# Two model blocks in fp32r on one core: the splits of the weights get the priority of instructions 400 places earlier

## Chip, cores and metric

The kernel runs on one core of one Trainium2 chip, in one launch. The metric is the device time of one execution in microseconds (us), lower is better. It is stated as the median over several runs.

## The reference

The program computes four layers of depth over 256 tokens of width 1024, in fp32. The first block has a state-space layer (SSD), a differential attention layer and a convolutional feed-forward network behind each of them; the second block has four gated feed-forward networks, a memory attention with a gated convolution in the first of its layers, and a forgetting attention with memory attention in the second. Cut to its skeleton:

```python
def first_block(x, ...):
    for i in range(2):
        h = rmsnorm(x, norm_mix_g[i])
        x = x + (ssd_mixer(h, ...) if i == 0 else diff_attention(h, ...))
        x = x + conv_ffn(rmsnorm(x, norm_ffn_g[i]), ...)      # D_FF = 2816
    return x

def second_block(x, mem, ...):
    mem_n = rmsnorm_2(mem, mem_norm)
    for l in range(2):
        # l == 1: keys, values and forget gates of x are made first
        x = x + 0.5 * swiglu(rmsnorm_2(x, ffn_norm[l, 0]), ...)  # D_FF_2 = 2816
        proj = rmsnorm_2(x, mix_norm[l]) @ w
        x = x + concatenate([token_mixer(proj), memory_attention(proj, mem_n)]) @ w_out
        x = x + 0.5 * swiglu(rmsnorm_2(x, ffn_norm[l, 1]), ...)
    return rmsnorm_2(x, final_norm)
```

Nearly all of the work is activations (256 x 1024) times weights. All weights together are about 309 MB in fp32, each used once.

## The kernel before

Activations lie transposed in SBUF, features on the partitions and the 256 tokens along a row. Every weight matmul is done in three: `mm3` (L252) multiplies the high half of the weights with the high half of the activations, the high half with the low half, and the low half with the high half, and adds all three up in one PSUM bank. For that each raw weight tile has to be split. `load` and `load_tiles` (L228, L233) issue one DMA from SP into a raw buffer `wr` (three of them, 2048 columns each). `split` (L240) then makes two tiles from 1024 columns of it or fewer: `wh`, a copy rounded to fp32r by ScalarE (ACT), and `wl`, the difference of raw and `wh`, by VectorE (DVE) or, in the state-space layer, every fourth time by GpSimd (POOL). `wh` and `wl` have five buffers each. A raw buffer is free again when all its low halves are made; a `wh` or `wl` buffer when the last matmul that reads it is through.

Three loops use this. `lin_T` (L290) takes two tiles of 128 output features at a time, 8 matmul triples each, into one of three PSUM buffers `psA`, and has it evacuated (for the state-space layer: DVE multiplies by the row norm, L394, ACT and DVE run a convolution of four taps, L886 and L889). `lin_N` (L315) makes outputs with tokens on the partitions. `lin_out` (L338) is the way back to 1024 features; it adds onto `X` (L366) and feeds the next norm.

The state-space layer has, per group of eight heads, a chain beside these loops: transposes on PE (L768), a copy `xn` (ACT, L770), decay factors `E` (PE L785, DVE L792, ACT L797, POOL L798), small matmuls (L815), the sum `y` (DVE L834), and then a gate with its own norm (POOL L842, ACT L843, POOL L384, DVE L850), transposes (L858) and the split of the result `yy` (L865, L866), which `lin_out` reads. The attention layer has rope chains (L993 to L1009) and heads (L1021 on).

These chains are generators. A running count `net.now` of estimated PE time says where in the source order each of their pieces is issued (`spawn`, `adv`, `resume`). That order gives each instruction a place number, its priority. A planner then goes through the program in a model of the machine and gives each engine, whenever it comes free there, the instruction with the lowest number among those that can run: inputs made, and a buffer free for the output. What comes out is one fixed list per engine, which the chip works through in order. So the number is a preference among what can run at the moment, not a place in the list.

Of the kernel before, what the change touches and what calls it, by code (L numbers as in the profile page):

```python
# [10 lines left out]
F32 = mybir.dt.float32  # L11
# [3 lines left out]
AF = mybir.ActivationFunctionType  # L15
ALU = mybir.AluOpType
# [84 lines left out]
class Net:  # L101
# [138 lines left out]
    def split(self, raw, c0, n):  # L240
        nc = self.nc
        hi = self.t(self.wh, [128, 1024], F32R, "wh")
        lo = self.t(self.wh, [128, 1024], F32R, "wl")
        nc.scalar.activation(out=hi[:, :n], in_=raw[:, c0:c0 + n], func=AF.Copy)  # L244
        self.cnt += 1
        pool = self.share and self.cnt % self.share == 0 and (self.norm is None or self.norm.done)
        eng = nc.gpsimd if pool else nc.vector
        eng.tensor_tensor(out=lo[:, :n], in0=raw[:, c0:c0 + n],  # L248
                          in1=hi[:, :n].bitcast(F32), op=ALU.subtract)
        return hi, lo  # L250

    def mm3(self, ps, wh, wl, xh, xl, first, last):  # L252
# [118 lines left out]
    def make_norm(self, gname, split=True, sq="act", pool=None, base=64):  # L371
        return Norm(self, gname, split, sq, self.xp if pool is None else pool, base)
# [30 lines left out]
class Norm:  # L403
    def __init__(self, net, gname, split, sq, pool, base):
        self.n, self.g, self.split = net, gname, split
        self.done = False
        self.sq = sq
        self.keep = None
        self.wait = 4.5
        self.acc = net.t(net.s2, [128, S], F32, "nacc")  # L410
        if split:
            self.xh, self.xl = Moving(net, pool, KD, "xx", base, (0,)).parts()
# [102 lines left out]
def next_norm(net, gname, split=True, pool=None, base=64):  # L515
    box = {}

    def after(m):
        if m == 0:
            box["n"] = net.make_norm(gname, split=split, pool=pool, base=base)  # L520
        box["n"].step(m)
    return box, after
# [1025 lines left out]
```

## Time and profile before

| | |
|---|---|
| median of 3 runs | 1797.99 us (1792.98 to 1803.73) |
| profiled execution, its own time | 1808.89 us |
| its span, first to last instruction | 1807.2 us |
| PE, DVE, ACT, POOL busy | 98%, 68%, 56%, 27% |
| mean granted TensorE clock | 0.994 |

Times in the rows are microseconds from the start of the span. PE is TensorE's matmuls, PEld its weight loads. Matmuls are pipelined and their ends are modelled, so that a busy PE can still run below its best rate; the number of matmuls in a stretch says more. A square bracket at the end of a row gives how long the engine was idle just before the instruction, and what ended that.

### The profile page before, as it was taken

The page shows a single profiled execution, that of the slowest core. Times are in us where ns is not written, and L with a number is a line of the kernel's source. Part 1 is how long each engine was busy: PE and PEld are TensorE (multiplying, and loading weights), DVE is VectorE, ACT ScalarE, POOL GpSimd, SP SyncE. Part 2 cuts the span into 40 slices and gives each one's busy share as a digit, 9 for nine tenths or more (in the row PEclk, how much of TensorE's full clock was granted, in tenths as well). Part 3 has the DMA queues.
Part 4 walks back from the last instruction along what each step waited for, and adds up shares of the span by engine and source line. Part 5 has one row for each costly group of instructions (what it writes and reads, how often), then busy time and mean ns, then how long its engine had stood idle before and what let it go on. Part 6 is the DMA issues. An engine that isn't in the chain of part 4 may idle for free.

```text
span 1807.2 us, 34773 instructions
## 1 busy us (share of the span) xinstructions
PE 1774.4 (98%) x14067; PEld 1708.8 (95%) x14067; DVE 1235.2 (68%) x1863; ACT 1015.7 (56%) x1661; POOL 490.9 (27%) x453
## 2 busy tenths in 40 slices
PE   8999999999999999999999999999999999999997
PEld 7887999998789999999999999999999998999997
DVE  6998789867777997655567775556655567575553
ACT  7667576646666665554455454455544455564443
POOL 3555234402111442043201223310043210023321
PEclk9999999999999999999999999999999999999999
DMA  6332655465226555655464475556555454265553
GB/s 233 118 139 81 212 178 186 158 195 206 94 100 228 187 180 162 208 199 187 152 221 143 140 233 187 180 163 199 195 199 186 157 206 164 82 222 187 180 162 103
DMA packets 76497, 312.12 MB, mean 173 GB/s; under 512 B 6192, under 2 KB 6320, under 8 KB 72624
## 3 DMA queue, kind: packets, MB, share of 16 engines
q1 hardware_dynamic: 76304, 309.89, 50.4%
q8 instruction: 111, 1.82, 0.4%
q14 instruction: 50, 0.41, 0.1%
q0 software_dynamic: 32, 0.00, 0.0%
HBM read 308.82 MB, written 1.05 MB: 171 GB/s over the span
## 4 chain that ended last, share of the span: by engine, by line
PE 86%; DVE 6%; POOL 2%; ACT 1%; issue 1%; DMA 1%; DVEq 0%; ACTq 0%; POOLq 0%
PE psA L254 26%; PE psA L256 25%; PE psA L255 25%; PE psA L329 2%; PE psA L327 2%; PE psA L328 2%; DVE wl L248 2%; DVE cvy L889 2%; POOL rs L384 1%; PE psM L1033 1%; ACT wh L244 0%; DVE E L792 0%; PE psM L1147 0%; PE psY L1178 0%; DMA wr<-memT 0%
## 5 line engine op out<-in xcount | busy, mean ns | idle before, releaser
L248 DVE TENSOR_TENSOR wl<-wr,wh 128x1024 fp32r<-128x1024 f32 (+3 forms) x651 | 719.7, 1108 | 389.9 <-ACT wh L244 387.2
L244 ACT ACTIVATE wh<-wr 128x1024 fp32r<-128x1024 f32 (+3 forms) x660 | 628.1, 955 | 491.4 <-PE psA L255 313.3
L256 PE MATMUL psA<-xx,wl 128*128 128x256 f32 x2752 | 775.6, 282 | 5.9 <-DVE wl L248 5.9
L254 PE MATMUL psA<-xx,wh 128*128 128x256 f32 x2752 | 779.7, 283 | 0.2 <-DVE pad L394 0.2
L255 PE MATMUL psA<-xx,wh 128*128 128x256 f32 x2752 | 773.6, 281 | 0.1
L256 PEld LDWEIGHTS psA<-xx,wl 128*128 128x128 f32 x2752 | 526.4, 191 | 7.4 <-DVE wl L248 6.9
L254 PEld LDWEIGHTS psA<-xx,wh 128*128 128x128 f32 x2752 | 518.8, 189 | 1.8 <-issue 0.5
L255 PEld LDWEIGHTS psA<-xx,wh 128*128 128x128 f32 x2752 | 518.5, 188 | 1.1 <-issue 0.5
L256 PE MATMUL psA<-gg,wl 128*128 128x256 f32 x1056 | 296.9, 281 | 0.0
L254 PE MATMUL psA<-gg,wh 128*128 128x256 f32 x1056 | 296.6, 281 | 0.0
L255 PE MATMUL psA<-gg,wh 128*128 128x256 f32 x1056 | 296.4, 281 | 0.0
L544 POOL TENSOR_TENSOR p<-s,t 128x256 f32<-128x256 f32 x132 | 184.0, 1394 | 367.8 <-ACT s L572 367.8
L256 PEld LDWEIGHTS psA<-gg,wl 128*128 128x128 f32 x1056 | 202.1, 191 | 0.0
L254 PEld LDWEIGHTS psA<-gg,wh 128*128 128x128 f32 x1056 | 198.2, 188 | 0.0
L255 PEld LDWEIGHTS psA<-gg,wh 128*128 128x128 f32 x1056 | 198.2, 188 | 0.0
L431 POOL TENSOR_TENSOR nacc<-nacc,sq 128x256 f32<-128x256 f32 x72 | 63.3, 879 | 487.2 <-ACT sq L376 486.4
L547 POOL TENSOR_TENSOR gg<-p,gg 128x256 fp32r<-128x256 f32 x132 | 109.5, 830 | 125.5 <-ACT gg L546 125.5
L546 ACT ACTIVATE gg<-p 128x256 fp32r<-128x256 f32 x132 | 54.2, 412 | 127.0 <-POOL p L544 126.9
L254 PE MATMUL psA<-yy,wh 128*128 128x256 f32 x384 | 107.8, 282 | 0.1
L255 PE MATMUL psA<-yy,wh 128*128 128x256 f32 x384 | 106.9, 279 | 0.3 <-DVE yy L1223 0.3
L256 PE MATMUL psA<-yy,wl 128*128 128x256 f32 x384 | 106.6, 278 | 0.0
L394 DVE TENSOR_TENSOR t<-psA,R 128x512 f32<-128x512 f32 (+1 forms) x104 | 69.4, 670 | 36.9 <-PE psA L256 35.5
(291 smaller groups left out, 1921.8 us busy)
## 6 DMA issues: line engine op xcount, KB each, us to landing
wr<-up SPq DMA_DIRECT2D x132, 1024.0 KB, 4.8
wr<-dn SPq DMA_DIRECT2D x96, 704.0 KB, 4.0
wr<-w_a SPq DMA_DIRECT2D x14, 1024.0 KB, 4.8
wr<-w_ssd SPq DMA_DIRECT2D x12, 1024.0 KB, 5.1
wr<-w_ain SPq DMA_DIRECT2D x12, 1024.0 KB, 4.8
wr<-w_ssdo SPq DMA_DIRECT2D x16, 512.0 KB, 4.4
wr<-w_z SPq DMA_DIRECT2D x7, 1024.0 KB, 4.7
wr<-w_ao SPq DMA_DIRECT2D x16, 384.0 KB, 3.2
```

The lines of the kernel that those rows point to most:

```text
L244: nc.scalar.activation(out=hi[:, :n], in_=raw[:, c0:c0 + n], func=AF.Copy)
L248: eng.tensor_tensor(out=lo[:, :n], in0=raw[:, c0:c0 + n], in1=hi[:, :n].bitcast(F32), op=ALU.subtract)
L254: mm(ps, lhsT=wh, rhs=xh, start=first, stop=False)
L255: mm(ps, lhsT=wh, rhs=xl, start=False, stop=False)
L256: mm(ps, lhsT=wl, rhs=xh, start=False, stop=last)
L327: mm(ps[b], lhsT=xh[:, k, xs], rhs=hi[:, c], start=k == 0, stop=False)
L328: mm(ps[b], lhsT=xl[:, k, xs], rhs=hi[:, c], start=False, stop=False)
L394: self.nc.vector.tensor_tensor(out=o, in0=p, in1=self.bc(R, n), op=ALU.mult)
L431: eng.tensor_tensor(out=self.acc, in0=self.acc, in1=sq, op=ALU.add)
L544: nc.gpsimd.tensor_tensor(out=p, in0=s, in1=t[:, 1], op=ALU.mult)
L546: nc.scalar.activation(out=gh[:, j], in_=p, func=AF.Copy)
L547: nc.gpsimd.tensor_tensor(out=gl[:, j], in0=p, in1=gh[:, j].bitcast(F32), op=ALU.subtract)
```

## The change

The two instructions of a split are issued inside a block that lowers the running place number by 400 and sets it back afterwards. All else keeps its number. The line that makes `wh` moves below the two lines that choose the engine for `wl`; those lines issue nothing.

```diff
         hi = self.t(self.wh, [128, 1024], F32R, "wh")
         lo = self.t(self.wh, [128, 1024], F32R, "wl")
-        nc.scalar.activation(out=hi[:, :n], in_=raw[:, c0:c0 + n], func=AF.Copy)
         self.cnt += 1
         pool = self.share and self.cnt % self.share == 0 and (self.norm is None or self.norm.done)
         eng = nc.gpsimd if pool else nc.vector
-        eng.tensor_tensor(out=lo[:, :n], in0=raw[:, c0:c0 + n],
-                          in1=hi[:, :n].bitcast(F32), op=ALU.subtract)
+
+        with self.tc.high_priority(400):
+            nc.scalar.activation(out=hi[:, :n], in_=raw[:, c0:c0 + n], func=AF.Copy)
+            eng.tensor_tensor(out=lo[:, :n], in0=raw[:, c0:c0 + n],
+                              in1=hi[:, :n].bitcast(F32), op=ALU.subtract)
         return hi, lo
```

## Rows read from the trace of the kernel before

**Rows 1.** Page, part 1: busy us (share of the span) and instructions of each engine.

```profile
PE 1774.4 (98%) x14067; PEld 1708.8 (95%) x14067; DVE 1235.2 (68%) x1863; ACT 1015.7 (56%) x1661; POOL 490.9 (27%) x453
```

**Rows 2.** Stretches: length, busy us (count) of PE, PEld, DVE, ACT, POOL; PEclk, DMA.

```profile
28.00:170.00 142.00, 129.00 (x874) 115.47 (x874) 132.67 (x229) 100.34 (x151) 71.80 (x44) 0.96 0.33 116
...
400.00:575.00 175.00, 170.09 (x1040) 142.65 (x1039) 126.16 (x303) 110.27 (x244) 33.33 (x34) 0.99 0.43 152
575.00:950.00 375.00, 375.00 (x3187) 375.00 (x3187) 259.55 (x332) 209.90 (x324) 110.16 (x105) 1.00 0.55 188
```

**Rows 3.** Waits of PE: who waited for what: us in total, times, longest us.

```profile
PE psA L256 <- DVE wl L248: 5.9, 4, 2.4
PE psM L785 <- ACT xn L770: 4.4, 1, 4.4
PE psM L1013 <- DVE qt L1009: 3.7, 3, 2.2
...
PE psA L329 <- DVE wl L248: 1.6, 2, 1.3
```

**Rows 4.** Chain of waits from 28 to 191 us, shares by line.

```profile
by line: DVE cvy L889 16.7%; DVE wl L248 10.5%; issue 7.0%; PE psA L254 5.7%; PE psA L256 5.6%; PE psA L255 5.4%; DVE E L792 4.6%; POOL E L798 3.7%; POOL y L842 3.4%; POOL rs L384 2.9%; DVE pad L394 2.6%; PE psY L815 2.6%; PE psM L785 2.4%;
```

**Rows 5.** Timeline of ACT and DVE, 34 to 76 us: start, us, instruction, count.

```profile
34.67 3.89 ACT L244 ACTIVATE wh<-wr 128x1024 fp32r<-128x1024 f32 x4
...
43.45 1.22 DVE L248 TENSOR_TENSOR wl<-wr,wh 128x1024 fp32r<-128x1024 f32 x1
...
64.76 2.25 DVE L248 TENSOR_TENSOR wl<-wr,wh 128x1024 fp32r<-128x1024 f32 x1
66.94 5.59 DVE L889 SCALAR_TENSOR_TENSOR cvy<-pad,cv,cvy 128x256 f32<-128x256 f32 x6
72.46 2.35 DVE L248 TENSOR_TENSOR wl<-wr,wh 128x1024 fp32r<-128x1024 f32 x2
```

**Rows 6.** Waits over the whole span: ACT before a split.

```profile
ACT wh L244 <- PE psA L255: 313.3, 303, 4.1
```

**Rows 7.** Timeline of PE: instructions before which PE stood idle.

```profile
44.73 0.55 PE L256 MATMUL psA<-xx,wl 128*128 128x256 f32 x1 [2.36 <-DVE wl L248]
...
73.72 0.39 PE L256 MATMUL psA<-xx,wl 128*128 128x256 f32 x1 [1.67 <-DVE wl L248]
...
129.66 0.50 PE L785 MATMUL psM<-cc,sel 64*128 64x256 f32 x2 [4.43 <-ACT xn L770]
...
190.70 1.29 PE L858 MATMUL psM<-ident,y 128*128 128x128 f32 x8 [0.68 <-DVE y L850]
```

**Rows 8.** Stretches at a granted clock (PEclk) of 0.50.

```profile
44.79:48.21 3.42, 3.42 (x16) 3.42 (x17) 3.41 (x4) 2.60 (x5) 2.02 (x1) 0.50 0.24 43
130.13:136.95 6.82, 6.82 (x27) 5.92 (x27) 6.13 (x17) 2.66 (x4) 3.64 (x3) 0.50 0.31 131
```

**Rows 9.** Timeline of DVE: its idle time in the state-space layer.

```profile
94.58 2.31 DVE L775 TENSOR_TENSOR xdt<-xn,NT 128x512 f32<-128x512 f32 x2 [2.22 <-ACT xn L770]
...
137.85 0.87 DVE L792 TENSOR_SCALAR E<-psM,NT 128x128 f32<-128x128 f32 x3 [1.59 <-PE psM L785]
140.92 5.41 DVE L889 SCALAR_TENSOR_TENSOR cvy<-pad,cv,cvy 128x256 f32<-128x256 f32 x6 [2.21 <-ACT cvy L886]
```

**Rows 10.** Timeline of DVE, 164 to 185 us: the last group's chain.

```profile
164.63 4.21 DVE L792 TENSOR_SCALAR E<-psM,NT 128x128 f32<-128x128 f32 x16
...
175.82 0.88 DVE L850 TENSOR_SCALAR y<-y,rs 128x512 f32<-128x512 f32 x2 [4.43 <-POOL rs L384]
...
182.70 1.31 DVE L248 TENSOR_TENSOR wl<-wr,wh 128x1024 fp32r<-128x1024 f32 x1 [0.42 <-ACT wh L244]
183.93 1.27 DVE L834 TENSOR_TENSOR y<-psY,xn 128x512 f32<-128x512 f32 x2
```

**Rows 11.** Timeline of POOL: its products for E.

```profile
62.02 6.12 POOL L798 TENSOR_TENSOR E<-E,cbm 128x512 f32<-128x512 f32 x4
...
169.09 6.03 POOL L798 TENSOR_TENSOR E<-E,cbm 128x512 f32<-128x512 f32 x4
```

## Prediction

> **What bounds the kernel now.** I read the page's busy shares first. PE is busy for 1774.4 us, 98% of the span, and DVE for 1235.2 [rows 1]. The profiled execution took 1808.89 us, its span of 1807.2 and 1.7 us around it; that is 10.9 us above the median of the three timed runs, 1797.99. I work out differences in the profiled execution and take them off the median.
>
> Second, the stretches [rows 2]. From 575 to 950 us (two feed-forward blocks and more) PE has work all the time: 375.00 of 375 us, 3187 matmuls, one every 117.7 ns. There a split that comes earlier can give nothing. What PE lacks lies in a few places: 13.0 of the 142 us from 28 to 170 (the state-space layer), 4.9 of the 175 us of the attention layer. In the first of these DVE is busy for 132.67 of 142 us, its idle time 9.3 us.
>
> Third, who PE waited for [rows 3]. Only two rows name the low half of a split (wl, line 248): 5.9 us in four waits and 1.6 us in two, 7.5 us together. The largest single wait, 4.4 us, is for the copy xn of line 770; 3.7 us are for the rope chain of the attention layer (line 1009).
>
> Fourth, the chain of waits from 28 to 191 us [rows 4]. The three PE lines of the weight matmuls hold 16.7% of it together; DVE alone holds 16.7% with the convolution (L889), 10.5% with wl and 4.6% with E. So in this layer the end is set by DVE's total work more than by any one wait of PE.
>
> Fifth, how late the splits are there [rows 5]. ACT makes four high halves back to back from 34.67 to 38.56 us. Every fourth low half goes to POOL, so the second of these four, done at 36.6, is for DVE at the latest; DVE takes its next low half at 43.45, 6.8 us later, and PE stands until 44.73 for it [rows 7]. From 66.94 to 72.46 DVE runs six convolution instructions and only then the low halves that PE stands for at 73.72. DVE takes older work first, and the low halves stand behind it. In the saturated blocks it is the other way round: ACT itself stands idle before the split, 313.3 us in 303 waits, until PE frees a buffer [rows 6]. There the split is already the first thing to run when it can.
>
> **The change part by part.** No instruction is added or removed; every high half on ACT and every low half on DVE or POOL gets a number 400 lower. A tile of 1024 columns makes some 27 instructions (24 matmuls, two halves, a load), so 400 places are about 15 tiles, while the wh and wl pools hold 5. The number therefore means "first whenever it can run", and the pools are the limit. SP's loads keep their numbers; a raw buffer is freed earlier by as much as its low half comes earlier.
>
> *Saturated blocks.* The split is already first [rows 6] and PE has no gap [rows 2]: 0. An eviction may stand behind one split of 1.22 us, while the three psA buffers cover more than one tile pair (48 matmuls of 117.7 ns, 5.6 us). If that cover were gone it would cost 1.2 us a pair; I take 0.
>
> *State-space layer, what goes.* [...] The wait of 4.43 us at 129.66 and the half clock of 6.82 us behind it (3.4 us) have another cause, the order on ACT; they go only if that order happens to change [rows 7, 8].
>
> *What is late next.* PE gains nothing at the end of the layer by this alone. At 190.70 it has already run out of other work and waits 0.68 us for the last head group's gated output, y of line 850 [rows 7]. What PE wins before that point it gives back there, unless the DVE chain that makes y comes earlier too. So the layer must be priced on DVE. Three terms:
> - DVE's own idle time where PE or ACT was late: 2.22, 1.59 and 2.21 us [rows 9], 6.0 together. The first comes after PE's waits for wl up to then (the one at 73.72 among them), the others after its stand at 129.66 [rows 7]. With PE earlier they can shrink to 0: -6.0. Lower end 0, since the second and third come from the ACT order.
> - More splits ahead of the last group's E. If PE is 7.5 us further on, it has freed 7.5/2.8 = 2.7 tiles more (24 matmuls of 117.7 ns are 2.8 us), so three more low halves of 1.22 us run before the 16 instructions of E at 164.63 [rows 5, 10]: +3.7. Ends 0 and five buffers, 6.1.
> - The end of the chain. DVE stands 4.43 us before line 850 for POOL's reciprocal root, until 175.82; later y of line 834 starts only when a low half of 1.31 us that began at 182.70 is through [rows 10]. Splits that ran in that hole would not stand in front later: -1.3. Ends 0 and -1.3.
>
> Sum for this layer: -6.0 + 3.7 - 1.3 = -3.6 us.
>
> *Attention layer.* PE's waits are for the rope chain, not for splits [rows 3]. Two low halves put ahead of that chain would cost 2 x 1.22 = 2.4 us; PE coming later or earlier may save half of a half-clock stretch like the first, 1.7. I take 0, nearest to the row that shows no wait for wl there. *Start.* The first split waits for its load in any case; a later one (3.89/4 = 0.97 us on ACT [rows 5]) could get in front of the scaled input: 0 to +1.0, taken as 0, since the next raw tiles arrive behind the input.
>
> [...] A low half that began at 64.76 took 2.25 us against 1.22 for the one at 43.45, while POOL ran its E products from 62.02 to 68.14 [rows 5, 11]. [...]
>
> All in all: 1808.9 - 3.6 = 1805.3 as profiled, and 1798.0 - 3.6 = 1794 us as timed. The likeliest case's own range takes the ends: -6.0 - 1.3 - 1.7 = -9.0 (1789) and 3.7 + 2.4 + 1.0 = +7.1 (1805).
>
> **The rivals.**
> One, nothing moves: the planner's order already has each split in front where it matters. For it: the 303 waits of ACT for a buffer [rows 6]. Against: the low half that lay ready for 6.8 us [rows 5]. Time 1798.
>
> Two, faster: PE's gains are kept. The wl waits go (7.5), the first half clock goes (1.7), and the ACT order behind the stand at 129.66 changes as well (4.4 + 3.4): 17.0 us, 1781. For it: each of these is PE standing with work loaded. Against: DVE is 93% busy in that layer and PE has no slack at 190.70.
>
> Three, slower: the last head group's chain is pushed back. With splits first, all five buffers are filled before E at 164.63, 5 x 1.22 = 6.1 us, and POOL's four E products of 6.03 us at 169.09 [rows 11] and the gate follow that much later, with PE out of work. The same in the attention layer, where two low halves stand ahead of each of two rope chains, 4 x 1.22 = 4.9. Together +11.0: 1809. It decides from the point where the added splits exceed the 6.0 us of DVE idle time that can be regained, that is at five of them. For it: PE's waits at 190.70 and for line 1009 show chains without slack. Against: splits are limited by the buffers that PE frees, and the hole of 4.43 us can take three of them.
>
> [...]
>
> **How the numbers follow.** Forecast 0.42, rival one 0.10, two 0.23, three 0.21, four 0.04. A measurement of this kernel can tell about 0.5% from no change, 9.0 us: 1789.0 to 1807.0. Below it lie rival two and 0.03 of the forecast, 0.26. Inside lie rival one and 0.38 of the forecast, 0.48. Above lie three, four and 0.01 of the forecast, 0.26. The range of 8 in 10 reaches past rivals two and three, 1778 to 1813: the lower end is 1781 with 3 us of the waits for line 1009 gone too, the upper end falls just short of rival four.
>
> **What would show it.** Right: PE's waits for wl fall from 7.5 us to under 2; low halves start within some 1.5 us of their high halves from 28 to 170 us; DVE idles under 5 us there; PE's wait for line 850 at the layer's end grows from 0.68 us to several; the stretches from 575 us on keep PE at full. Wrong: the layer's end, the last transposes of line 858, moves by over 9 us either way, or PE gets gaps in a feed-forward block because an eviction stands behind a split.

## The result and the profile after

The change makes the kernel slower. After it takes 1815.07 us (median of 16 runs, 1801.76 to 1831.17), before 1792.45 us on the same chip (16 runs, 1781.66 to 1803.86): a ratio of 1.0122, 95% interval 1.0099 to 1.0146, or 18 to 26 us. (The ratio leaves out the run of 1831.17 us, which lies over 1.5% above the fastest of its kernel.) I had forecast 1794 us and a range up to 1813. The profiled execution of after happens to be the fastest of its 16 (1801.76 us, span 1800.0), that of before (1808.89 us) is slower than any of its 16. The two spans say nothing about the difference; it has to be read stage by stage.

Lines of the changed kernel stand mostly two further down than before: `wh` is L249, `wl` L250, the matmuls of `mm3` L256 to L258. Part 1 of its page:

```profile
PE 1752.1 (97%) x14067; PEld 1681.3 (93%) x14067; DVE 1232.5 (68%) x1863; ACT 1016.0 (56%) x1661; POOL 486.5 (27%) x453
```

The three stretches of [rows 2] in the trace of after, same columns:

```profile
28.00:170.00 142.00, 127.14 (x852) 114.71 (x850) 119.62 (x209) 90.81 (x137) 62.83 (x39) 0.94 0.33 117
400.00:575.00 175.00, 165.46 (x1006) 136.28 (x1005) 122.59 (x295) 106.55 (x239) 32.72 (x31) 1.00 0.40 137
575.00:950.00 375.00, 373.41 (x3265) 372.80 (x3263) 267.77 (x343) 216.98 (x334) 112.71 (x108) 1.00 0.58 199
```

In the state-space layer PE stands more (14.9 of 142 us, 13.0 before), runs at a lower clock (0.94, 0.96 before) and gets 852 matmuls done in place of 874. DVE is busy for 119.62 us where it was 132.67: what I had expected to be the limit now idles for 22.4 us in place of 9.3.

Who PE waits for, over the whole span (answers to [rows 3]):

```profile
PE psM L1015 <- DVE qt L1011: 6.2, 5, 1.8
PE psM L787 <- ACT xn L772: 6.0, 2, 3.6
PE psY L817 <- POOL E L800: 4.3, 3, 2.3
PE psA L256 <- DVE pad L396: 2.7, 1, 2.7
PE psM L452 <- DVE nacc L433: 2.5, 1, 2.5
...
PE psA L258 <- DVE wl L250: 0.3, 1, 0.3
PE psA L331 <- DVE wl L250: 0.3, 1, 0.3
```

The waits for low halves are gone, 0.6 us in place of 7.5. The change does what it says: between 28 and 170 us the low halves, taken in order, start 0.8 us on average after the high halves end, where it was 7.0 us. But PE now waits longer for other things: for xn 6.0 in place of 4.4, for POOL's E 4.3 in place of 0.5, for the rope chain's qt 6.2 in place of 3.7, and for an eviction (pad, 2.7).

DVE's two longest waits from 28 to 204 us say where its time went:

```profile
DVE wl L250 <- ACT wh L249: 9.4, 9, 3.2
DVE nv L848 <- ACT zs L845: 7.1, 2, 4.1
```

The first of these was, before, from 28 to 192 us:

```profile
DVE wl L248 <- ACT wh L244: 0.9, 3, 0.4
```

A low half that stands early in DVE's fixed list has DVE wait for its high half, 9.4 us in all, in which DVE runs nothing else.

**Where the 22 us are.** A mixer's stage is taken from the last matmul of the feed-forward block ahead of it (for the first one from the span's start) to its own last matmul on `yy` in `lin_out`. The state-space stage lasts 238.3 us, 228.7 before; the attention stage 157.8, 152.1 before; the two mixers of the second block 122.6 and 122.6, 122.2 and 120.6 before. That is 9.6 + 5.7 + 0.4 + 2.0 = 17.7 us, at the lower end of the interval; PE's stands in the feed-forward blocks, at the norms between a mixer and the block behind it, add some 2 us in all. (The blocks' lengths differ for another reason, see the last section.)

In the state-space layer the last gate transposes (L860) end at 203.6 us, 192.0 before. (The stage itself grows by less, 9.6 us: behind the gate after needs 34.7 us and before 36.7.) The whole stretch from 28 us to that end, in the trace of after:

```profile
28.00:203.60 175.60, 156.98 (x1034) 140.26 (x1033) 145.07 (x249) 113.09 (x170) 81.55 (x52) 0.94 0.33 115
```

Before:

```profile
28.00:192.00 164.00, 150.32 (x1024) 134.74 (x1024) 146.88 (x248) 113.97 (x170) 83.12 (x52) 0.97 0.35 119
```

PE's idle time grows from 13.7 to 18.6 us, +4.9. The stretches at a granted clock of 0.50 grow from 10.2 [rows 8] to 20.5 us. In them 256-column matmuls start 0.21 us apart, elsewhere 0.11 to 0.12; I count half of each stretch as lost, an estimate from the clock of 0.50: +5.1. Together +10.0 of the 11.6. Two of the new stretches:

```profile
98.48:101.89 3.41, 3.41 (x14) 2.96 (x15) 3.41 (x6) 1.06 (x1) 1.99 (x2) 0.50 0.32 132
122.38:125.79 3.41, 3.41 (x18) 3.41 (x18) 1.22 (x4) 0.05 (x1) 0.00 (x0) 0.50 0.02 5
```

Each begins 0.6 us after a stand of PE ends: 3.63 us until 97.87, and 2.31 us until 121.79. In the traces of e1 and e10 (below), whose splits in this layer are ordered as with the change or nearly so, the stretches from 50.70 to 142.86 us stand at the same places within 1 us; so they are no chance of one execution. How the first of these stands comes about is the clearest case of the mechanism. First POOL's timeline of after, around 95 us:

```profile
91.77 1.27 POOL L844 TENSOR_TENSOR y<-y,zs 128x512 f32<-128x512 f32 x1 [6.35 <-DVE y L836]
93.01 2.35 POOL L250 TENSOR_TENSOR wl<-wr,wh 128x1024 fp32r<-128x1024 f32 x1
95.32 1.26 POOL L844 TENSOR_TENSOR y<-y,zs 128x512 f32<-128x512 f32 x1
```

ACT at the same time:

```profile
96.61 0.63 ACT L845 ACTIVATE zs<-y 128x512 f32<-128x512 f32 x1 [2.81 <-POOL y L844]
97.15 0.19 ACT L845 ACTIVATION_READ_ACCUMULATOR zs<-y 128x1 f32 x1
97.24 1.06 ACT L772 ACTIVATE xn<-psM 128x512 f32<-128x512 f32 x2
```

DVE, which had nothing to do for 4.15 us:

```profile
97.37 0.17 DVE L848 TENSOR_SCALAR nv<-ss 128x2 f32<-128x2 f32 x1 [4.15 <-ACT zs L845]
```

And PE:

```profile
92.79 0.71 PE L770 MATMUL psM<-ident,xsT 128*128 128x128 f32 x5
93.43 0.50 PE L787 MATMUL psM<-cc,sel 64*128 64x256 f32 x2
93.86 0.39 PE L256 MATMUL psA<-xx,wh 128*128 128x256 f32 x1
97.87 0.50 PE L787 MATMUL psM<-cc,sel 64*128 64x256 f32 x2 [3.63 <-ACT xn L772]
98.30 0.45 PE L257 MATMUL psA<-xx,wh 128*128 128x256 f32 x1
98.55 0.42 PE L258 MATMUL psA<-xx,wl 128*128 128x256 f32 x1
```

POOL puts a low half of 2.35 us between the two products of the first group's gate. ACT's second square needs the second product and waits 2.81 us for it. Behind the square in ACT's list stand the copies xn, whose input is there since 93.5 us: they need nothing of the gate, they only stand behind it. PE's next matmul in its list needs the PSUM buffer that xn frees, and the weight matmuls behind it in the list start only after it. When PE starts again, its 256-column matmuls follow one another at 0.21 us in place of 0.12. So one split of 2.35 us stands at the head of a stand of 3.63 us and a half-clock stretch of 3.41 us; e19 below takes it away and shows what goes with it.

### The profile page after: what moved, and what is told of

Read it like the earlier page. It is cut to its first block, busy times and chain, and to the rows that moved or that the text cites. A ratio compares the mean times of both kernels' runs of the same rounds, so it can differ in the third digit from the quotient of the medians.

```text
span 1800.0 us, 34777 instructions
## 1 busy us (share of the span) xinstructions
PE 1752.1 (97%) x14067; PEld 1681.3 (93%) x14067; DVE 1232.5 (68%) x1863; ACT 1016.0 (56%) x1661; POOL 486.5 (27%) x453
## 4 chain that ended last, share of the span: by engine, by line
PE 83%; DVE 4%; ACT 2%; issue 1%; DMA 1%; POOL 1%; DVEq 0%; ACTq 0%; POOLq 0%
PE psA L257 25%; PE psA L256 24%; PE psA L258 24%; PE psA L329 2%; PE psA L331 2%; PE psA L330 2%; DVE wl L250 2%; ACT wh L249 1%; PE psM L1035 1%; POOL rs L386 1%; DVE cvy L891 0%; PE psY L1180 0%; DMA wr<-memT 0%; DMA wr<-w_aout 0%; PE psM L1149 0%
## 5 line engine op out<-in xcount | busy, mean ns | idle before, releaser
L250 DVE TENSOR_TENSOR wl<-wr,wh 128x1024 fp32r<-128x1024 f32 (+3 forms) x651 | 719.1, 1107 | 402.8 <-ACT wh L249 396.8
L249 ACT ACTIVATE wh<-wr 128x1024 fp32r<-128x1024 f32 (+3 forms) x660 | 628.7, 956 | 487.8 <-PE psA L257 316.2
L256 PE MATMUL psA<-xx,wh 128*128 128x256 f32 x2752 | 772.9, 281 | 3.1 <-DVE pad L396 2.7
L258 PE MATMUL psA<-xx,wl 128*128 128x256 f32 x2752 | 769.5, 280 | 0.3 <-DVE wl L250 0.3
L256 PEld LDWEIGHTS psA<-xx,wh 128*128 128x128 f32 x2752 | 520.0, 189 | 4.8 <-ACT xdt L725 2.9
L258 PEld LDWEIGHTS psA<-xx,wl 128*128 128x128 f32 x2752 | 521.6, 190 | 1.5 <-DVE wl L250 0.5
L257 PE MATMUL psA<-gg,wh 128*128 128x256 f32 x1056 | 293.3, 278 | 0.0
L256 PE MATMUL psA<-gg,wh 128*128 128x256 f32 x1056 | 293.1, 278 | 0.0
L258 PE MATMUL psA<-gg,wl 128*128 128x256 f32 x1056 | 293.1, 278 | 0.0
L258 PEld LDWEIGHTS psA<-gg,wl 128*128 128x128 f32 x1056 | 199.0, 188 | 0.0
L256 PEld LDWEIGHTS psA<-gg,wh 128*128 128x128 f32 x1056 | 198.4, 188 | 0.0
L256 PE MATMUL psA<-yy,wh 128*128 128x256 f32 x384 | 108.1, 282 | 0.2 <-ACT yy L1224 0.2
L258 PE MATMUL psA<-yy,wl 128*128 128x256 f32 x384 | 106.9, 279 | 0.0
L569 DVE SCALAR_TENSOR_TENSOR t<-pad,cv,t 128x256 f32<-128x256 f32 x176 | 93.9, 591 | 0.0
```

The lines of the kernel that those rows point to most:

```text
L250: eng.tensor_tensor(out=lo[:, :n], in0=raw[:, c0:c0 + n], in1=hi[:, :n].bitcast(F32), op=ALU.subtract)
L256: mm(ps, lhsT=wh, rhs=xh, start=first, stop=False)
L257: mm(ps, lhsT=wh, rhs=xl, start=False, stop=False)
L258: mm(ps, lhsT=wl, rhs=xh, start=False, stop=last)
L569: nc.vector.scalar_tensor_tensor(out=t[:, h], in0=pd[:, h, tap:tap + S], scalar=net.col(f"fw{conv}{tap}", c), in1=t[:, h], op0=ALU.mult, o ...
```

## The experiments

All times are medians of 4 to 16 runs against the kernel before on the same chip in the same set. "Gate" is the end of the last gate transposes; the column behind it has PE's idle time and the half-clock time from 28 us to there, and the last column the same two for the attention stage. Stages come from one profiled execution each. For the state-space layer, kernels with nearly the same order there agree: 228.7, 228.1 and 228.7 us for before, e2 and e16, 238.3 and 239.1 for the change and e10.

| kernel | ratio to before (95%) | state-space stage | gate | PE idle, half | attention stage: PE idle, half |
|---|---|---|---|---|---|
| before | 1 | 228.7 | 192.0 | 13.7, 10.2 | 152.1: 4.4, 3.4 |
| the change | 1.0122 (1.0099 to 1.0146) | 238.3 | 203.6 | 18.6, 20.5 | 157.8: 9.5, 0.0 |
| e1_ssd_only | 1.0043 (1.0010 to 1.0075) | 234.6 | 198.9 | 16.0, 17.1 | 154.1: 4.4, 6.8 |
| e2_not_ssd | 1.0065 (1.0032 to 1.0098) | 228.1 | 192.5 | 13.5, 10.2 | 158.2: 8.6, 3.4 |
| e3_high_only | 1.0110 (1.0057 to 1.0163) | 236.3 | 199.6 | 17.5, 20.5 | 164.1: 11.7, 10.2 |
| e4_low_only | 1.0105 (1.0066 to 1.0144) | 235.6 | 198.6 | 18.5, 20.5 | 162.3: 10.0, 6.8 |
| e8_chain_over | 1.0149 (1.0105 to 1.0193) | 238.5 | 199.5 | 19.0, 10.2 | 158.8: 10.9, 3.4 |
| e6_chain_first | 1.0148 (1.0105 to 1.0191) | 241.0 | 200.3 | 22.6, 3.4 | 162.5: 10.9, 13.7 |
| e5_off40 | 1.0034 (0.9997 to 1.0072) | 235.2 | 199.5 | 16.3, 17.1 | 152.0: 3.0, 6.8 |
| e7_later60 | 1.0025 (0.9991 to 1.0060) | 232.8 | 196.1 | 11.8, 17.1 | 154.0: 4.3, 6.8 |
| e10_pool_old | 1.0161 (1.0123 to 1.0198) | 239.1 | 204.4 | 19.3, 20.5 | 157.8: 9.5, 0.0 |
| e11_inputs_over | 1.0086 (1.0057 to 1.0116) | 239.5 | 203.9 | 17.1, 23.9 | 154.4: 4.1, 6.8 |
| e12_inputs_first | 1.0079 (1.0051 to 1.0108) | 234.5 | 198.9 | 16.3, 20.5 | 156.4: 4.2, 10.2 |
| e13_inputs40 | 1.0093 (1.0057 to 1.0130) | 237.2 | 201.6 | 16.5, 23.9 | 159.2: 3.9, 17.1 |
| e14_first12 | 1.0008 (0.9979 to 1.0036) | 234.6 | 199.0 | 15.1, 20.5 | 152.5: 3.1, 6.8 |
| e15_after12 | 1.0080 (1.0045 to 1.0115) | 240.8 | 203.5 | 19.4, 23.2 | 156.9: 3.2, 17.1 |
| e16_first8 | 1.0017 (0.9989 to 1.0044) | 228.7 | 193.1 | 14.1, 10.2 | 150.5: 4.4, 0.0 |
| e19_split28 | 1.0147 (1.0106 to 1.0188) | 235.0 | 200.3 | 20.7, 10.2 | 158.8: 7.4, 6.8 |

The attention stage is better read by PE's idle time than by its length. It holds half-clock stretches that differ from profile to profile: 3.4 us with before, none with the change, 17.1 us in e15, where the numbers of the attention layer are those of before. The stage with before, with the change, in e11 and in e15 (length, PE busy, and so on as in [rows 2]):

```profile
416.20:568.30 152.10, 147.70 (x854) 120.74 (x854) 108.44 (x282) 97.01 (x225) 30.76 (x29) 0.99 0.39 136
421.50:579.30 157.80, 148.26 (x854) 119.08 (x853) 109.39 (x282) 97.01 (x225) 30.97 (x29) 1.00 0.38 130
427.70:582.10 154.40, 150.28 (x854) 121.75 (x853) 109.12 (x283) 96.28 (x225) 30.59 (x29) 0.98 0.36 132
423.10:580.00 156.90, 153.71 (x854) 125.10 (x854) 109.53 (x284) 97.33 (x226) 30.53 (x29) 0.95 0.36 132
```

PE stands there for 3.0 to 4.4 us in the kernels that leave the attention layer's splits at or near their old numbers (e6 apart, which lowers the numbers of the chains with their matmuls and has 10.9), and for 7.4 to 11.7 us in those that lower them by 400 (e11 apart, with 4.1).

**Which layers, and which half.** Theory A: splits overtake the head groups' chains and the rope chains, so that PE runs out of those. Theory B: the loss is in the dense blocks, where evictions stand behind splits. A1 and A2 put it on the low halves (DVE) or the high halves (ACT).

e1 and e2 put the lower number around the state-space layer's splits alone, or around all others:

```diff
-        with self.tc.high_priority(400):
+        with self.tc.high_priority(400) if self.share else ExitStack():
```

> The lowered number is used for the splits of the state-space layer's input weights (w_ssd, w_z) alone. Theory A (chains of the state-space, attention and mixer layers overtaken by splits, so that PE's list waits for them): PE's waits up to the layer's last yy matmul rose from 27.5 to 42.1 us in the two profiles, so this alone gives +12 to +16 us against the kernel before, the rest of the +22 us lies behind the layer. Theory B (the loss is in the dense blocks, evictions behind splits or a slower pace of PE's matmuls there): 0 to +4 us here.

> The other half: the lowered number for all splits but those of w_ssd and w_z. Theory A: +7 to +12 us (attention's PE waits 5.3 to 12.0 us, the two mixers 0.5 to 8.4 us in the two profiles), with the state-space layer up to its last gate as before and no dense block longer than before at the same pace. Theory B: +18 us or more.

e3 takes the low half out of the block, e4 in the same way the high half:

```diff
         with self.tc.high_priority(400):
             nc.scalar.activation(out=hi[:, :n], in_=raw[:, c0:c0 + n], func=AF.Copy)
-            eng.tensor_tensor(out=lo[:, :n], in0=raw[:, c0:c0 + n],
-                              in1=hi[:, :n].bitcast(F32), op=ALU.subtract)
+        eng.tensor_tensor(out=lo[:, :n], in0=raw[:, c0:c0 + n],
+                          in1=hi[:, :n].bitcast(F32), op=ALU.subtract)
```

> Only the high halves on ACT get the lowered number. Theory A1 (the low halves on DVE are what overtakes the chains, since DVE is the engine without slack in the state-space layer): 0 to +5 us, PE still waits for low halves about as often as before (7.5 us). Theory A2 (the high halves at the head of ACT's list are what holds the chains back, as in PE's waits for the copy xn, 6.0 us after the change): +12 us or more.

> Only the low halves on DVE and POOL get the lowered number. Theory A1: +15 to +22 us, nearly the whole loss, with PE's waits for low halves gone. Theory A2: under +8 us.

Measured: +7.7 us (e1) and +11.6 us (e2). A is nearer than B: e2 loses in attention (+6.1) and nothing in the state-space layer, e1 the other way round (+5.9, and +2.0 in attention, where PE's idle time stays at 4.4), and the dense blocks keep to their lengths. But e1 falls short of what A said, and together with the later splits that layer loses 9.6. A1 and A2 both fall: either half alone brings nearly the whole loss, with less of it in the state-space layer and more in attention than the two together.

**Putting the chains first again.** e8 adds to the change, e6 to the kernel before, a lower number for the generators' pieces:

```diff
-        d = next(a[1], None)
+        with self.tc.high_priority(800):   # e6: 400, and no block around the splits
+            d = next(a[1], None)
```

> The change, and the generator pieces (the SSD head chain, the rope and head chains) get a number 800 lower, so that they stand ahead of the splits again. Theory A (the splits overtake these chains, and PE then waits for the chains' results): most of the loss goes, 1785 to 1800 us where the kernel before takes 1791; the last gate transposes of the SSD layer end by 195 us (192.0 before, 203.6 with the change), the attention stage takes at most 154 us (152.1 and 157.8). Theory C (the order before is one that fits, and any other order of this size costs some 1%): 1803 to 1818, the gate transposes after 197 us.

> The splits keep their numbers as before; only the generator pieces get a number 400 lower. The opposite of the change in the order of chain and split. Theory A: as fast as the kernel before or faster, 1780 to 1795, since the chains are what PE runs out of; PE's waits for wl may grow beyond the 7.5 us of before. Theory C: 1803 to 1815.

Both are 27 us slower than before: A as I had put it falls. The pieces hold PE's own matmuls too, and the longest waits are now those of such matmuls for their inputs, in e8 as in e6. PE's waits of e6 from 28 to 202 us:

```profile
PE psM L759 <- ACT CT L895: 6.2, 3, 3.2
PE psM L860 <- DVE y L852: 4.2, 2, 3.0
PE psM L827 <- POOL xw L779: 3.0, 3, 1.1
```

So two more runs left the numbers of PE's instructions alone and lowered those of DVE, ACT and POOL inside the generators only (e11 with the change, 800; e12 without it, 400; e13 without it, 40). A wrapper around those three engines does it while `boost` is set:

```diff
+        self.boost = True
         d = next(a[1], None)
+        self.boost = False
...
+            with self.net.tc.high_priority(800):
+                return f(*a, **k)
```

> The change, and in the generators the instructions on DVE, ACT and POOL alone get a number 800 lower; the chains' matmuls and transposes on PE keep theirs. Theory A2 (the splits hold up the makers of the chains' inputs, and the earlier matmuls of e8 spoiled its cure): 1785 to 1802 beside 1795 of before, the gate transposes of the SSD layer end by 196 us, the attention stage takes at most 154 us. Theory C (any order far from that of before costs 1%): 1808 to 1825.

> The kernel before, splits with their old numbers; in the generators the instructions on DVE, ACT and POOL get a number 400 lower, PE's keep theirs. Theory A2: 1780 to 1796 beside 1795, the waits for xn, E and qt smaller than before. Theory C: 1805 to 1820.

> As the run before, with 40 in place of 400. Theory A2: a part of that gain, 1785 to 1796. Theory C, by the size of the step: +2 to +8, as the splits moved by 40 or 60 did.

e11 settles the attention stage: PE's idle time there is 4.1 us, as before, against 9.5 with the change (154.4 us of stage against 157.8), with PE's wait for qt down from 6.2 to 2.9 us. PE's longest wait from 400 to 585 us, with the change:

```profile
PE psM L1015 <- DVE qt L1011: 6.2, 5, 1.8
```

The same in e11, where instructions of a wrapped engine carry the wrapper's line, L112:

```profile
PE psM L1044 <- DVE qt L112: 2.9, 2, 1.5
```

There the loss is the makers of the rope chain's inputs standing behind splits. For the rest A2 falls: e11 is still some 15 us slower than before, and the state-space layer stays as long as with the change (239.5): its first waits in e11 are for xsT (7.0 us) and for an eviction zs (5.0). e12 and e13 lose some 15 us without any change to the splits. For e12 that is what theory C said; for e13, with its step of 40, C had +2 to +8 us, and the loss is twice the upper end of that.

**How far, and the other way.** e5 uses 40 places in place of 400, e7 minus 60 (later splits):

```diff
-        with self.tc.high_priority(400):
+        with self.tc.high_priority(40):   # e7: -60
```

> The change with 40 places in place of 400, some 1.5 tiles of 27 instructions. Theory A in the form that the five wh and wl buffers, not the number, set how far a split gets ahead: 1805 to 1817, nearly as the change. Theory A in the form that the loss grows with the number of chain pieces that are overtaken: 1792 to 1802. Theory C: 1803 to 1818.

> The splits get a number 60 higher, so they come later than before. Theory A: the chains lose nothing, but PE waits for low halves: the waits for wl in the SSD layer grow from 7.5 us to 15 or more, 1795 to 1810. Theory C: 1803 to 1818 without the waits for wl growing by as much. If it is faster than the kernel before, the splits of before were too early already.

Both lie 4 to 6 us above before by the ratio, but their intervals reach 1. With the change's 400 places the loss is clear, and in attention PE's idle time goes from 3.0 us (e5) to 9.5; so the buffers are not the only limit. In the state-space layer even 40 places cost 6.5 us in the profile. In e7 PE's waits for wl don't grow, as theory A had it, but fall to 4.0 us. From 28 us to the gate PE stands less than before (11.8 us, 13.7) with more half clock (17.1 us, 10.2), and the gate's end is 4.1 us later. The table leaves out what comes ahead of 28 us, and in e7 that matters. The first 28 us with before and in e7, same columns:

```profile
0.00:28.00 28.00, 24.50 (x111) 17.65 (x112) 15.40 (x31) 17.31 (x32) 11.83 (x21) 1.00 0.82 301
0.00:28.00 28.00, 20.35 (x79) 14.72 (x80) 15.66 (x30) 17.12 (x30) 11.08 (x21) 0.88 0.75 270
```

PE's longest wait of e7 in them:

```profile
PE psY L256 <- ACT wh L249: 4.0, 1, 4.0
```

A later split makes PE stand 4.0 us for a high half at the start, 6.8 us at half clock are there too, and PE has 79 matmuls done in place of 111. e4, e5, e6, e8 and e10 to e14 also have 3.4 to 10.2 us at half clock ahead of 28 us, before and the change none; a part of their longer stages can come from there.

**Where the state-space layer's loss starts.** e10 leaves only POOL's low halves at their old numbers:

```diff
-            eng.tensor_tensor(out=lo[:, :n], in0=raw[:, c0:c0 + n],
-                              in1=hi[:, :n].bitcast(F32), op=ALU.subtract)
+            if not pool:
+                eng.tensor_tensor(out=lo[:, :n], in0=raw[:, c0:c0 + n],
+                                  in1=hi[:, :n].bitcast(F32), op=ALU.subtract)
+        if pool:
+            eng.tensor_tensor(out=lo[:, :n], in0=raw[:, c0:c0 + n],
+                              in1=hi[:, :n].bitcast(F32), op=ALU.subtract)
```

> The change, but the low halves that POOL makes (every fourth in the SSD layer) keep their old numbers. Theory P (a POOL low half of 2.4 us now stands between the products of the gate, as at 93.01 us with the change, and holds DVE, ACT and PE one after the other): the SSD layer's end falls from 203.6 to 197 us or less, the attention stage stays at 158, the time is 5 to 7 us under the change's. Theory Q (the low halves on DVE and the high halves on ACT do the same by themselves): the end stays at 200 to 204, the time within 3 us of the change's.

The stages don't change: POOL's low half stands between the same two products (93.79 to 96.14 us there). So it isn't the lower number of this low half that puts it there. What does is not shown: DVE has made the input of the second product by 93.08 us, 0.7 us before the low half starts, so in the trace that product could have gone first.

e14, e15 and e16 lower the number for the first twelve splits of the layer (all before 32 us), for those from the thirteenth on, and for the first eight (all before 25 us):

```diff
-        with self.tc.high_priority(400):
+        with self.tc.high_priority(400 if self.share and self.cnt <= 12 else 0):
```

> Only the first twelve splits of the SSD layer get the number 400 lower, all later ones keep theirs. With the change PE is 4.9 us ahead of before at the 300th weight matmul of the layer (69 us), and loses that and more from 93 us on. Theory E (the early gain is real, and what loses it is that later splits overtake the chains): the gain lasts, the last gate transposes end at 187 to 192 us (192.0 before, 203.6 with the change), -5 to 0 us against before. Theory F (PE running ahead is itself what makes the first group's chain late, since its evictions and convolutions then fill DVE): the same loss at 93 to 104 us, the end at 196 to 201 us, +3 to +8 us.

> The complement within the SSD layer: its splits from the thirteenth on get the number 400 lower, the first twelve and all other layers keep theirs. Theory E: the full loss of that layer, the end at 198 to 204 us, +6 to +12 us. Theory F: little, 192 to 196 us, 0 to +4 us.

> As the first of these, with eight in place of twelve; these come before any chain of a head group is due. Theory E: -4 to 0 us, the end at 188 to 192. Theory F: a loss from 93 us on again, if PE is ahead by more than 2 us at the 240th weight matmul. Theory C (any other order costs, whatever it moves): the end at 195 to 201 us all the same, +3 to +8 us.

The 4.9 us in the first of these counts weight matmuls, and the order of 512-column and 256-column ones differs. By all columns that PE has streamed, the change is 1.3 us ahead at 70 us, level at 80 and 1.2 ahead at 90, so the early gain was small to begin with. e16 ends as before (228.7 us), so theory C in its strict form, that any departure costs, falls. e14 moves four splits more, whose low halves start between 27 and 32 us, and the layer is 5.9 us longer; its time is not measurably slower (+1.4 us, -3.8 to +6.5). e15 loses 12.1. Both together (e1) lose 5.9. The loss is not a sum over splits: each set of numbers gives another list from that point on, and what decides which stands it has is not shown. Neither E nor F describes that.

e19 takes away the one low half at 93.01 us: the 28th split's goes to DVE.

```diff
-        pool = self.share and self.cnt % self.share == 0 and (self.norm is None or self.norm.done)
+        pool = (self.share and self.cnt % self.share == 0 and self.cnt != 28
+                and (self.norm is None or self.norm.done))
```

> The change, with one low half (the 28th split) made by DVE in place of POOL. With the change POOL makes it from 93.01 to 95.36 us between the two products of the first group's gate; ACT's second square and behind it the copies xn wait for that, PE stands 3.63 us until 97.87, and a half-clock stretch follows. DVE is idle at that time. Theory G (that product held up is what starts the loss): the stand of PE for xn near 97 us falls to 1.5 us or less, the half-clock stretch behind it is gone, the last gate transposes end by 200 us (203.6 with the change), 2 to 6 us under the change's time. Theory C (the list changes from there on and another stand takes its place): the stand for xn shrinks, but the end stays at 201 to 206 us and the time within 3 us of the change's.

POOL's timeline of e19 (lines one further down than with the change):

```profile
91.88 3.49 POOL L845 TENSOR_TENSOR y<-y,zs 128x512 f32<-128x512 f32 x2 [6.35 <-DVE y L837]
```

PE's:

```profile
94.77 0.49 PE L788 MATMUL psM<-cc,sel 64*128 64x256 f32 x2 [1.15 <-DVE cbm L764]
96.66 0.50 PE L788 MATMUL psM<-cc,sel 64*128 64x256 f32 x2 [1.40 <-ACT xn L773]
```

The chain of causes is confirmed at this place: the stand of 3.63 us becomes 1.15 and 1.40, and no half clock follows. But theory C has a part in it: other stands take its place. The 1.15 us are for cbm, which now stands behind the same low half on DVE:

```profile
92.33 1.92 DVE L251 TENSOR_TENSOR wl<-wr,wh 128x1024 fp32r<-128x1024 f32 x1
94.17 0.55 DVE L764 TENSOR_TENSOR cbm<-psM,m 128x384 f32<-128x384 f32 x1
```

And with that low half beside them POOL's two products take 3.49 us, where they took 1.27 and 1.26. Up to the gate PE's idle time grows, from 18.6 to 20.7 us, and its half-clock time falls from 20.5 to 10.2. Two of the three stretches that are gone followed stands of 2.31 and 2.33 us with the change; e19 has stands of 2.20 and 2.77 us in their place, and no half clock behind them. So not all of the 3.3 us by which the gate's end comes earlier (200.3 us, where theory G said by 200) goes back to the one low half. The time doesn't show a gain: 26 us above before, interval 19 to 34, not below the change's. One execution's stage and a median over others differ by several us here (see the last section).

## Why the prediction was wrong

*What held.* The saturated blocks cost next to nothing: in the trace of after a block inside takes 181.7 or 187.0 us, no eviction shows as a gap, and only the norms ahead of two blocks add the 2 us named above. The waits for wl fell from 7.5 us to 0.6, the lag of low halves to 0.8 us on average. PE gains nothing by that alone, as I had argued. Two of my signs of being right failed: from 28 to 170 us DVE idles for 22.4 us and not under 5, and PE's wait for the gated output at the layer's end is 0.6 us and not several. The sign of being wrong came: the last gate transposes moved by 11.6 us.

*The step that failed: DVE's idle time, the term -6.0.* I took 2.22 + 1.59 + 2.21 us [rows 9] as time that would be regained once PE was earlier, and offset it with +3.7 for three low halves. The sum treated DVE as a pool of work whose order is free. Its list is fixed: a low half that is early in it stops DVE until ACT has made the high half (9.4 us, 0.9 before), ACT's late squares stop it too (7.1 us, 1.9 before), and its idle time rose from 17.1 to 30.5 us up to the gate's end. The same shows on ACT (xn, its input there since 93.5 us, starts behind the square at 97.24) and on PE (in the stand of 3.63 us until 97.87 the weight matmul of 98.30, whose piece of `wh` the one at 93.86 had read already, does not run ahead of the chain matmul). So the term of -6.0 came out as +13.4 us of idle time, and in place of -3.6 us the layer's stage gave +9.6.

*The half clock.* I counted 1.7 us as a gain, half of the stretch of 3.42 us at 44.79 [rows 8]. That is an estimate of mine, and no run shows the term. In its place the stretch came back longer (6.83 us from 50.70, in a stand of 2.72 us for an eviction), and four more of 3.41 us each came behind new stands. Half of the growth, by estimate 5.1 us, is nearly half of the 11.6 us by which the gate's end moved. I had priced stands at their own length alone wherever a new one could arise.

*Attention, taken as 0.* It lost 5.7 us, with 5.1 us more of PE's stands (4.4 to 9.5). I had bounded it by two low halves, 2.4, in the forecast, and by 4.9 in rival three. The reason for 0, that no wait for wl shows there, was no reason: what PE lacked was what the earlier splits pushed back. The two mixers of the second block, 2.4 us together, had no term at all.

*Rival three* had the direction and the mechanism, a chain pushed back by splits, and its 4.9 us for the rope chains are close to the 5.7 found. Its sum, +11.0, is half of the loss of 22 us. It put the rest at the last head group (6.1 us). There the trace has 4.7 of it: e1, where the splits behind the layer keep their numbers, has its gate's end at 198.9 us, the change at 203.6, and there PE stands 1.77 us for POOL's E until 192.72, which it doesn't in e1. But most of the layer's loss arises earlier, in the middle groups, and doubles by the half clock, which that rival left out. Rival four adds 5 x 1.03 = 5.2 us to that sum, for low halves that DVE makes beside POOL's E; no run shows this term. One low half beside E took 2.25 us, where another took 1.22 [rows 5, 11], and that POOL was the cause is not shown; up to the gate's end DVE's busy time fell from 146.9 to 145.1 us.

That rival four's 1814 us lie next to the 1815 measured is luck: they stand for +16 us on the 1797.99 of the first three runs, and over 16 runs before takes 1792.45.

*What stays open.* Why the order before is better in the state-space layer than the others tried: all fifteen that differ from it there beyond 25 us have that stage longer by 4 to 12 us, with splits earlier or later, chains first or last (for e5, e7 and e14 the timed runs don't tell the kernel from before). What is shown is how such a loss arises in one place (e19) and of what it consists (stands and half clock), not a rule by which a number or an offset would avoid it. Nor is it shown which stands bring half clock: up to the gate the 4.43 us until 129.66 before and the 3.63 us until 97.87 with the change did, but of the stands of 1.67 to 2.72 us in these two traces some did and some did not (with the change the 1.77 us until 192.72 did, before the 1.74 us until 88.55 did not). No version tried is faster than the kernel before.

## What to carry to other kernels

A priority in a planner that writes fixed lists is not a head start at run time: it puts an instruction in front of others that could have run while it waits (DVE waited 9.4 us for high halves here, 0.9 before). Before moving work ahead, list what stands behind it on its engine and for which matmul that is the input; price every new stand of PE together with the half clock that follows stands of its length in the traces at hand, as a cost that can but need not come. And where the engine's time is spread over chains without slack, a gain in one wait is not a gain in the stage until the stage's end has moved (PE's waits for wl fell by 6.9 us here, and the state-space stage grew by 9.6).

## What the runs showed of the hardware

In the traces of before and after each dense block runs at one of two paces, at a granted clock of 1.00 in both. Two stretches of 50 us of after, in two blocks, PE busy throughout:

```profile
1150.00:1200.00 50.00, 50.00 (x427) 50.00 (x426) 25.71 (x27) 23.69 (x36) 17.18 (x18) 1.00 0.48 161
1350.00:1400.00 50.00, 50.00 (x440) 50.00 (x439) 28.19 (x27) 24.94 (x37) 20.04 (x19) 1.00 0.55 194
```

427 or 440 instructions in the same time; the 256-column matmuls start 117.6 or 114.2 ns apart, for a whole block, and a block takes 187.0 or 181.7 us, 5.3 us apart. Before's profiled execution ran all its blocks at 117.6 ns, after's all but one at 114.2; which blocks run at which pace differs between the profiles here (one of each kernel), also between kernels whose splits in these blocks have the same numbers (before, e1, e14, e15, e16). With six such blocks that is, by estimate, up to 32 us between two executions, of the size of the spread of the 16 runs of before (22 us) and of after (29); that the pace makes that spread is not shown, and what sets the pace was not tested. It is why a difference of 20 us had to be read from stages, and why two profiled spans, 1807.2 before and 1800.0 after, had the sign wrong: 17.7 us of the mixers and 2 of the norms, less 5 times 5.3 us of pace, make -6.8, and the spans differ by -7.2.
